# A decoder layer on one core: the attention denominators' reciprocals are spread by VectorE and DRAM transfers in place of TensorE transposes

## The chip, the cores and the metric

The kernel runs on one core of a Trainium2 chip. The metric is device time in microseconds (us) of one execution. Before the change it is 1200.84 us, the median of three runs (1200.32 to 1201.92).

## What is computed

One layer of a hybrid trunk on x of 1024 tokens by 1024 channels, float32. An RMS norm and one input projection feed two mixers: a gated DeltaNet (4 heads) and a dilated attention (8 heads of 64). Their outputs go side by side through an output projection and a residual add; then a second norm, a gated MLP with a short convolution, another residual add and the final norm.

The change is in the attention. Each of its three branches lets a query see keys at a stride; the branches are merged by their denominators, so that per head and query there is one sum of products and one sum of weights:

```python
num_tot = wts[0][..., None] * nums[0] + wts[1][..., None] * nums[1] + wts[2][..., None] * nums[2]
den_tot = wts[0] * dens[0] + wts[1] * dens[1] + wts[2] * dens[2]
out = num_tot / den_tot[..., None]
```

The kernel does all three branches as one softmax over the union of their keys (a mask holds the log of how many branches see a key), and multiplies the products by `1/den`.

## The kernel before

Activations lie with channels on the partitions and tokens along the free axis. TensorE ("PE") does the projections as dense products of split operands, three 128x512 matmuls for each 128 channels (`mm3`: `xhi,whi`, `xlo,whi`, `xhi,wlo`), and between them the pieces of whatever else is ready. A small planner (class `Weave`) runs the parts of the layer as generators: each yields an estimate of when its operands are ready, and the planner lets the one with the lowest level go on. TensorE's instructions carry a token that keeps them in the order in which they were written; the other engines' and the DMA queue's order is made by a scheduler from the order of writing, simulated times and priorities. Calls through `uv` and `ua` are VectorE ("DVE") and ScalarE ("ACT") calls with a high priority.

The attention works on two heads at a time (`pi`, 4 of them) and on half of the tokens (`hh`), which makes 8 groups, numbered 0 to 7 here. A group has four blocks of 128 queries (`u` = 0 to 3), handled in two pairs, so there are 16 pairs, numbered 0 to 15. A pair goes through three steps, and `advance` runs a step of three pairs at a time, in this order: the denominators of the older pair (`spread`), the turning of the newer one (`turn`), the values of the older one (`values`), and the scores of the next (`scores`). When the older pair is the second of its group, `merge_classes` adds the far keys, and `give` multiplies the group's products by the spread reciprocals and stores them.

- `scores` / `softmax`: products `ps<-kT,qT` in PSUM; DVE masks and takes the minimum (`sm<-ps,mk`, with `mx`), ACT takes the exponentials, which also gives the denominators `den`, two columns of the little tile `mx` (one for each head; queries are on the partitions).
- `turn`: `sm` is transposed on TensorE in 64x64 tiles (`ps<-ident,sm`, line 197; the array is used in 64 rows), and DVE and ACT copy the result to `pt` and `pb`. DVE then inverts `den` in place (`RECIPROCAL mx<-mx`), and GpSimd ("POOL") copies each of the two columns 64 times to a 128x128 tile `rd`.
- `spread`, one step later: TensorE transposes the pair's two `rd` tiles (`ps<-ident,rd`, 128x128, whole array), so that 1/den lies along the free axis on all partitions, in the PSUM bank `rb`. After the group's second pair ACT copies the bank to `rT` (`rT<-ps`).
- `give`: DVE multiplies `oT<-ps,rT`, and SyncE's queue ("SP") stores `mixer<-oT`. The last group's `oT` stays in SBUF.

Around the attention TensorE does dense columns: first `a` columns (queries and keys of later heads, stored through `apark<-aqkv`), then `z` columns, which end on DVE as `xr`, `zz` and `og`. Their weights come as `wst<-in_wi` on the SP queue, are rounded by ACT (`whi<-wst`), and the rest is made by POOL (`wlo<-wst,whi`). The SP queue also brings each pair of heads' operands (`qT`, `kT`, `vn`, `vc`). It issues in order: an issue that waits for a semaphore holds up those behind it.

Of the kernel before, what the change touches and what calls it, by code (L numbers as in the profile page):

```python
# [7 lines left out]
F32 = mybir.dt.float32  # L8
# [7 lines left out]
P = 128  # L16
# [131 lines left out]
def hybrid_layer(tc, I, out):  # L148
    nc = tc.nc
    wv = Weave()  # L150
    ve = Engine(wv, nc.vector, "vector", 0.07, 0.00105)
    ac = Engine(wv, nc.scalar, "scalar", 0.12, 0.00085)

    uv = Engine(wv, nc.vector, "vector", 0.07, 0.00105, first=tc.high_priority)
    ua = Engine(wv, nc.scalar, "scalar", 0.12, 0.00085, first=tc.high_priority)
    po_ = Engine(wv, nc.gpsimd, "gpsimd", 0.15, 0.0021)
    sy = Engine(wv, nc.sync, "sync", 0.05, 0.00142, 2.2)
# [5 lines left out]
    sp = es.enter_context(tc.tile_pool(name="sp", bufs=1))  # L163
    pp_ = es.enter_context(tc.tile_pool(name="pp", bufs=2, space=PSUM))
    dp = es.enter_context(tc.tile_pool(name="dp", bufs=1, space=DRAM))

    def tile_(pool, shape, dt, name, tag, bufs):
        return wv.slot(pool.tile(list(shape), dt, name=name, tag=tag, bufs=bufs), tag, bufs)
# [3 lines left out]
    def A(name, tag, dt=F32, shape=(P, 1024)):  # L172
        if tag in TURNS:
            i = turns[tag] = turns.get(tag, -1) + 1
            tag = TURNS[tag][i % len(TURNS[tag])]
        return tile_(lp, shape, dt, name, tag, SLOTS[tag])
# [19 lines left out]
    def tp(dst, src, idt=None, us=0.11):  # L196
        tc.stamp_issue_order_token(nc.tensor.transpose(dst, src, ident if idt is None else idt).ins, TOKEN)  # L197
        wv.product(us, dst, src)
# [60 lines left out]
    vpark = dp.tile([S, 512], F32, name="vpark")  # L259
    qpark = dp.tile([H, P, S], F32, name="qpark")  # L260
    atpark = dp.tile([H, P, S], F32, name="atpark")
    xpark = dp.tile([KT, P, S], F32, name="xpark")
    upark = dp.tile([FT, P, S], F32, name="upark")

    def bank(tag, name="ps"):
        return tile_(pp_, (P, 512), F32, name, tag, 2)
# [677 lines left out]
    HALVES = (slice(0, 64), slice(64, 128))  # L944

    def attention():
        for h in range(2):
            yield from wv.until(("c", h, NCH - 1))
        mk = A("mk", "go", shape=(P, 448))
        sy.dma_start(mk, I["mk"])  # L950
        for h in range(H):
            yield from wv.until(("o", h))
        for g in range(2):
# [43 lines left out]
        def ready_to_turn(pair):  # L997
            return max(wv.need(it["sm"], slack=t) for it, t in zip(pair, TSLACK))

        def turn(pair):  # L1000
            pts = A("pt", "dv*", shape=(P, 2, 2, 256))
            for b, (it, tag) in enumerate(zip(pair, ("asc", "atr"))):
                sm, near, far, u, den = it["sm"], it["near"], it["far"], it["u"], it["den"]
                nn, nf = near // P, -(-far // P)
                pt = it["pt"] = pts[:, b]
                pps = [bank(tag) for _ in range(2)]
                pvs = [pp.rearrange("p (e i t) -> p e i t", e=2, t=64) for pp in pps]
                for e in range(2):
                    for i in range(nn + nf):
                        o = far + i * P if i < nn else (i - nn) * P  # L1010
                        for pv, rr in zip(pvs, HALVES):
                            tp(pv[:, e, i, :], sm[rr, e, o:o + P], ident[rr, rr], 0.055)
                copies = uv.tensor_copy, lambda dst, src: ua.activation(dst, src, AF.Copy)
                for pv, rr, copy in zip(pvs, HALVES, copies):
                    copy(pt.rearrange("p e (i t) -> p e i t", t=P)[:, :, :nn, rr], pv[:, :, :nn, :])
                    for i in range(nf):
                        rows = min(it["far"] - i * P, P)
                        copy(it["pb"][i][:rows, :, u, rr], pv[:rows, :, nn + i, :])
                rd = it["rd"] = tile_(sp, [P, P], F32, "rd", ("r0", "r1", "w0", "w1")[u], 1)
                uv.reciprocal(den, den)  # L1020
                po_.tensor_copy(rd.rearrange("p (e d) -> p e d", e=2), den[:, :, None].to_broadcast([P, 2, 64]))

        def spread(pair):
            g = pair[0]["g"]
            yield wv.need(g["rb"], *[it["rd"] for it in pair])
            for it in pair:
                tp(g["rb"][:, it["u"] * P:(it["u"] + 1) * P], it["rd"])
            if pair[1]["u"] == 3:
                g["rT"] = tile_(sp, [P, 512], F32, "rT", "t2", 2)
                ac.activation(g["rT"], g["rb"], AF.Copy)  # L1030

        def values(pair):
            po = pair[0]["g"]["po"]
            yield wv.need(po, pair[0]["pt"], slack=-PSLACK)
            for it in pair:
                u = it["u"]
                for i in range(it["near"] // P):
                    for e, er in enumerate(HALVES):
                        mm(po[er, u * P:(u + 1) * P], v8(it["vn"])[:, it["k0"] // P + i, er],
                           it["pt"][:, e, i * P:(i + 1) * P], 0.11, u == 0 and i == 0, False, skip_group_check=True)  # L1040

        def merge_classes(g):
            vcv = g["vc"].rearrange("p (b c d) -> p b c d", b=2, c=4)
            po, hh = g["po"], g["hh"]
            yield wv.need(*g["pb"], slack=-PSLACK)


            parts = (((0, 128, 0), (1, 64, 2)) if hh else ((0, 64, 2),))
            for b, rows, u in parts:
                for c in range(4):  # L1050
                    for e, er in enumerate(HALVES):
                        mm(po[er].rearrange("p (u t) -> p u t", u=4)[:, u:, 32 * c:32 * c + 32],
                           vcv[:rows, b, c, er], g["pb"][b][:rows, e, u:, 32 * c:32 * c + 32], 0.11 - 0.028 * u,
                           False, c == 3 and b == hh, skip_group_check=True)

        def give(g):
            po, hh = g["po"], g["hh"]
            oT = tile_(sp, [P, 512], F32, "oT", "t2", 2)
            by = [t.rearrange("p (n c u) -> p n c u", n=4, c=4) for t in (po, g["rT"])]
            ve.tensor_tensor(oT.rearrange("p (n u c) -> p n c u", n=4, c=4), *by, op=OP.mult)  # L1060
            if g["pi"] < 3 or hh == 0:
                sy.dma_start(mixer[4 + g["pi"]][:, half(hh)], oT)
            else:
                last["oT"] = oT
            if hh == 1:
                wv.done.add(("o", 4 + g["pi"]))
# [4 lines left out]
        def advance(pair):  # L1071
            older, newer = pipe
            if newer is not None:
                yield ready_to_turn(newer)
            if older is not None:
                g = older[0]["g"]
                if older[0]["u"] == 0:
                    g.update(po=bank("ch"), rb=bank("ch"))
                yield from spread(older)
            if newer is not None:  # L1080
                turn(newer)
            if older is not None:
                yield from values(older)
                if older[1]["u"] == 3:
                    yield from merge_classes(g)
                    give(g)
            if pair is not None:
                yield from scores(pair, 0.3 if older is None else SSLACK)
            pipe[:] = newer, pair

        for pi in range(4):
            q, k, vn, vc = cur
            for hh in range(2):
                if hh == 1 and pi < 3:
                    yield from wv.until(("a", pi + 1, 1))
                    cur = att_load(pi + 1)
                pb = [A("pb", "qa", shape=(P, 2, 4, P)) for _ in range(1 + hh)]
                if pi == 3 and hh == 1:
                    wv.done.add("last group")
                for rows, b in (((slice(96, 128), 0), (slice(32, 64), 1)) if hh else ((slice(32, 64), 0),)):  # L1100
                    po_.memset(pb[b][rows, :, 0 if b < hh else 2, :], 0.0)
                g = dict(pb=pb, hh=hh, pi=pi, vc=vc)
                for u in (0, 2):
                    yield from advance([dict(n=4 * hh + i, u=i, q=q, k=k, vn=vn, pb=pb, g=g)
                                        for i in (u, u + 1)])
        for _ in range(2):
            yield from advance(None)
# [516 lines left out]
    for h in range(H):  # L1624
        wv.add(1, chain(h))
    wv.add(5, attention())
    wv.add(8, out_proj())
    wv.add(0, mixer_splits())
# [62 lines left out]
```

## Time and profile before

| | |
|---|---|
| median of the runs | 1200.84 us |
| the profiled execution's own time | 1200.36 us |
| its span, first to last instruction | 1198.6 us |
| granted TensorE clock, mean | 0.997 |
| TensorE busy | 1187.5 us, 7050 matmuls |
| VectorE / ScalarE / GpSimd busy | 915.1 / 574.8 / 89.8 us |
| attention, first turn to last merge | 322.7 to 442.8 us |

The profile is of one execution. Between its span and its time lie 1.8 us. A row of the timeline has the start and duration in us, the engine, the line, the operation, and output and inputs by the program's names; `x24` at its end means that 24 consecutive ones are merged; square brackets give the idle time of the engine before it and what ended that. PEld is TensorE's weight load, SPq the issue of a DMA on SyncE's queue. Matmuls overlap, so the distance of two starts tells what one takes, not its duration.

### The profile page before, as it was taken

How to read it: one execution, taken by the hardware profiler on the slowest of the kernel's cores; microseconds unless marked ns; L12 is line 12 of the kernel's file. 1: busy time of each engine (PE TensorE's matmuls, PEld its weight loads, DVE VectorE, ACT ScalarE, POOL GpSimd, SP SyncE). 2: the span in 40 equal slices, each digit the busy share in tenths (PEclk: the TensorE clock that was granted, in tenths of full speed). 3: DMA queues.
4: the chain of work that ended last, by engine and by line, in shares of the span. 5: the costliest groups of instructions: out<-in, count | busy, mean ns of one | idle time of the engine just before them, and what ended most of it. 6: DMA issues, size and time to landing. Idle time of an engine off the chain costs nothing.

```text
span 1198.6 us, 18324 instructions
## 1 busy us (share of the span) xinstructions
PE 1187.5 (99%) x7050; PEld 983.7 (82%) x7050; DVE 915.1 (76%) x1450; ACT 574.8 (48%) x1126; POOL 89.8 (7%) x100
## 2 busy tenths in 40 slices
PE   9999999999999999999999999999999999999997
PEld 7888888888777778888888888888888888888886
DVE  7683975665355566777989888989898889999875
ACT  7275345355454443655544544445445454434441
POOL 0212010214311120000000000000000000000000
PEclk9999999999999999999999999999999999999998
DMA  7435234436634204543213223131222398557414
GB/s 237 107 95 150 85 109 127 152 113 183 224 95 124 73 28 128 180 154 110 88 54 104 90 70 106 53 106 60 99 90 69 109 371 292 192 157 229 160 53 141
DMA packets 85798, 154.80 MB, mean 129 GB/s; under 512 B 21168, under 2 KB 36304, under 8 KB 85712
## 3 DMA queue, kind: packets, MB, share of 16 engines
q1 hardware_dynamic: 84848, 152.85, 39.1%
q8 instruction: 55, 0.90, 0.3%
q10 hardware_dynamic: 864, 0.79, 0.2%
q14 instruction: 31, 0.25, 0.1%
HBM read 117.68 MB, written 35.93 MB: 128 GB/s over the span
## 4 chain that ended last, share of the span: by engine, by line
PE 95%; DVE 2%; ACT 2%; issue 1%; DMA 0%; POOL 0%; POOLq 0%; DVEq 0%; SPq 0%; ACTq 0%
PE ps L193 45%; PE pa L193 20%; PE dw L193 17%; PE pc L193 10%; PE ps L197 3%; DVE kT L142 1%; ACT sm L144 0%; DMA xt<-in_xT 0%; DVE x1h L142 0%; ACT whi L142 0%; PE pd L193 0%; DVE zz L142 0%; ACT dec L142 0%; DVE xr L142 0%; DVE rstdB L142 0%
## 5 line engine op out<-in xcount | busy, mean ns | idle before, releaser
L193 PE MATMUL dw<-pr 128*128 128x512 f32 (+1 forms) x984 | 211.3, 376 | 0.0
L193 PEld LDWEIGHTS dw<-pr 128*128 128x128 f32 x984 | 176.7, 188 | 33.6
L193 PE MATMUL ps<-xhi,whi 128*128 128x512 f32 x384 | 157.7, 411 | 0.3 <-ACT xhi L144 0.3
L193 PE MATMUL ps<-xhi,wlo 128*128 128x512 f32 x384 | 150.3, 391 | 0.0
L193 PE MATMUL ps<-xlo,whi 128*128 128x512 f32 x384 | 148.4, 390 | 0.0
L193 PE MATMUL pa<-T,pair 128*128 128x512 f32 x528 | 127.0, 389 | 0.0
L193 PEld LDWEIGHTS pa<-T,pair 128*128 128x128 f32 x528 | 99.0, 188 | 20.6
L193 PEld LDWEIGHTS ps<-xhi,whi 128*128 128x128 f32 x384 | 72.5, 189 | 19.6 <-issue 5.6
L193 PEld LDWEIGHTS ps<-xhi,wlo 128*128 128x128 f32 x384 | 72.4, 188 | 15.7
L193 PEld LDWEIGHTS ps<-xlo,whi 128*128 128x128 f32 x384 | 72.3, 188 | 12.5
L142 ACT ACTIVATE u<-pa 128x512 f32<-128x512 f32 x44 | 26.3, 598 | 107.2 <-PE pa L193 107.2
L142 DVE SCALAR_TENSOR_TENSOR y<-xu,fcw,y 128x1023 f32<-128x1023 f32 (+1 forms) x44 | 56.4, 1281 | 22.1 <-ACT y L142 22.0
L142 ACT ACTIVATE whi<-wst 128x1024 fp32r<-128x1024 f32 x36 | 38.2, 1063 | 65.4 <-PE ps L193 54.3
L193 PE MATMUL pa<-B,A 128*128 128x512 f32 x264 | 63.4, 389 | 0.0
L193 PE MATMUL pa<-T,S 128*128 128x512 f32 x264 | 63.4, 389 | 0.0
L193 PE MATMUL pc<-B,pair 128*128 128x512 f32 x264 | 63.4, 389 | 0.0
L193 PE MATMUL pc<-T,S 128*128 128x512 f32 x264 | 63.4, 389 | 0.0
L142 DVE TENSOR_TENSOR wst<-wst 128x512 f32<-128x512 f32 x88 | 60.5, 688 | 0.9
L193 PE MATMUL ps<-B,pair 128*128 128x512 f32 x252 | 60.5, 389 | 0.0
L142 POOL TENSOR_TENSOR rs<-rs,mhalf 128x2 f32<-128x2 f32 (+2 forms) x4 | 4.7, 1187 | 738.4 <-DVE rs L144 738.4
L142 ACT ACTIVATE pr<-wd 128x1024 fp32r<-128x1024 f32 x33 | 34.9, 1058 | 49.5 <-PE dw L193 37.0
L144 ACT ACTIVATE sm<-sm,mx 128x128 f32<-128x128 f32 (+7 forms) x64 | 35.4, 556 | 48.2 <-DVE mx L144 48.2
(248 smaller groups left out, 2411.1 us busy)
## 6 DMA issues: line engine op xcount, KB each, us to landing
wst<-in_wu SPq DMA_DIRECT2D x44, 512.0 KB, 3.7
wd<-in_wd SPq DMA_DIRECT2D x44, 512.0 KB, 4.5
upark<-y SPq DMA_DIRECT2D x22, 512.0 KB, 3.6
wst<-in_wi SPq DMA_DIRECT2D x21, 512.0 KB, 3.8
r<-upark SPq DMA_DIRECT2D x11, 512.0 KB, 7.5
r<-upark SPq DMA_DIRECT2D x22, 256.0 KB, 7.5
wa<-in_wd SPq DMA_DIRECT2D x22, 256.0 KB, 3.3
wst<-in_wv SPq DMA_DIRECT2D x8, 512.0 KB, 3.7
```

The lines of the kernel that those rows point to most:

```text
L142: return getattr(eng, op)(*a, **kw)
L144: return getattr(eng, op)(*a, **kw)
L193: tc.stamp_issue_order_token(nc.tensor.matmul(dst, lhs, rhs, start=start, stop=stop, **kw).ins, TOKEN)
L197: tc.stamp_issue_order_token(nc.tensor.transpose(dst, src, ident if idt is None else idt).ins, TOKEN)
```

## The change

For groups 0 to 6 the reciprocals of both pairs go to eight columns of a 128x32 tile `dn` (two of them, in turn; the other columns hold 1.0). After the group's second pair DVE transposes `dn` to `dt` in 32x32 blocks, so that four blocks of 8 rows by 32 tokens stand on partitions 0, 32, 64 and 96. Four transfers put these side by side in DRAM as 8 rows of 128 tokens (`ddram<-dt`), and two transfers read them back, one for each head, each to 64 partitions (`rT<-ddram`). `spread` then does nothing for these groups, and `rb` is not reserved. Group 7 keeps the old way.

```diff
+    ddram = dp.tile([7, 8, P], F32, name="ddram")
...
+        dns = [tile_(sp, [P, 32], F32, "dn", f"dn{i}", 1) for i in range(2)]
+        for t in dns:
+            po_.memset(t, 1.0)
...
+                g = it["g"]
+                if g["n"] < 7:
+                    uv.reciprocal(dns[g["n"] % 2][:, 2 * u:2 * u + 2], den)
+                    continue
                 rd = it["rd"] = tile_(sp, [P, P], F32, "rd", ("r0", "r1", "w0", "w1")[u], 1)
                 uv.reciprocal(den, den)
                 po_.tensor_copy(rd.rearrange("p (e d) -> p e d", e=2), den[:, :, None].to_broadcast([P, 2, 64]))
+            g = pair[0]["g"]
+            if g["n"] < 7 and pair[1]["u"] == 3:
+                dt = tile_(sp, [P, 32], F32, "dt", "dt", 2)
+                ve.transpose(dt, dns[g["n"] % 2])
+                to = ddram[g["n"]]
+                for b in range(4):
+                    sy.dma_start(to[:, 32 * b:32 * b + 32], dt[32 * b:32 * b + 8, :])
+                rT = g["rT"] = tile_(sp, [P, 512], F32, "rT", "t2", 2)
+                for e, er in enumerate(HALVES):
+                    src = to.rearrange("(u e) t -> e u t", e=2)[e]
+                    sy.dma_start(rT[er].rearrange("p (u t) -> p u t", u=4),
+                                 bass.AP(tensor=src.tensor, offset=src.offset, ap=[[0, 64]] + list(src.ap)))
 
         def spread(pair):
             g = pair[0]["g"]
+            if g["n"] < 7:
+                return
...
-                    g.update(po=bank("ch"), rb=bank("ch"))
+                    g.update(po=bank("ch"))
+                    if g["n"] == 7:
+                        g.update(rb=bank("ch"))
...
-                g = dict(pb=pb, hh=hh, pi=pi, vc=vc)
+                g = dict(pb=pb, hh=hh, pi=pi, vc=vc, n=2 * pi + hh)
```

In the order of instructions this shows at three places. On TensorE, the turn of pair 1 (group 0), with the last dense matmuls ahead of it (`xhi`, `xlo` by `whi`, `wlo`); before:

```order
L193 MATMUL ps<-xhi,whi 128x512
L193 MATMUL ps<-xlo,whi 128x512
L193 MATMUL ps<-xhi,wlo 128x512
L197 MATMUL ps<-ident,rd 128x128 x2
L197 MATMUL ps<-ident,sm 128x64 x24
L193 MATMUL ps<-pt,vn 64x128 x6
```

and now:

```order
L193 MATMUL ps<-xhi,whi 128x512
L193 MATMUL ps<-xlo,whi 128x512
L193 MATMUL ps<-xhi,wlo 128x512
L197 MATMUL ps<-ident,sm 128x64 x24
L193 MATMUL ps<-pt,vn 64x128 x6
```

Two transposes are gone, and nothing else moved. The same holds at turns 1 to 14, so 28 transposes are gone in all; the dense matmuls ahead of each turn are as many as before.

On the SP queue, from the issue of weights ahead of group 0's transfers to group 1's; before:

```order
L142 DMA wst<-in_wi 128x1024
L142 DMA qT<-apark 128x1024
L142 DMA mixer<-oT 128x512
L142 DMA apark<-aqkv 128x1024
L142 DMA vn<-vpark 32x8x128
```

and now:

```order
L142 DMA wst<-in_wi 128x1024
L142 DMA qT<-apark 128x1024
L142 DMA ddram<-dt 8x32 x4
L142 DMA rT<-ddram 64x4x128 x2
L142 DMA mixer<-oT 128x512
L142 DMA ddram<-dt 8x32 x4
L142 DMA rT<-ddram 64x4x128 x2
L142 DMA apark<-aqkv 128x1024
L142 DMA vn<-vpark 32x8x128
```

Six transfers stand ahead of each group's store. For the later groups they also stand ahead of the next `apark<-aqkv` (groups 3 and 4) and of `wst<-in_wo` (group 6); group 2's come right behind a load of weights, `wst<-in_wi`.

On VectorE, at the last pair's turn (pair 15), where `xr`, `zz` and `og` are the end of a `z` column; before:

```order
L144 RECIPROCAL mx<-mx 128x2
L144 COPY pt<-ps 128x4x64
L144 COPY pb<-ps 128x2x64
L144 COPY pb<-ps 32x2x64
L144 COPY pt<-ps 128x4x64
L144 COPY pb<-ps 128x2x64
L144 COPY pb<-ps 64x2x64
L142 TENSOR_TENSOR oT<-ps,rT 128x4x4x32
L142 TENSOR_TENSOR xr<-ps,rstdB 128x512
L142 SCALAR_TENSOR_TENSOR zz<-zz,xr 128x1024
L142 TENSOR_TENSOR og<-og,zz 128x1024
```

and now:

```order
L144 RECIPROCAL mx<-mx 128x2
L142 TENSOR_TENSOR xr<-ps,rstdB 128x512
L142 SCALAR_TENSOR_TENSOR zz<-zz,xr 128x1024
L144 COPY pt<-ps 128x4x64
L144 COPY pb<-ps 128x2x64
L144 COPY pb<-ps 32x2x64
L142 TENSOR_TENSOR og<-og,zz 128x1024
L144 COPY pt<-ps 128x4x64
L144 COPY pb<-ps 128x2x64
L144 COPY pb<-ps 64x2x64
L142 TENSOR_TENSOR oT<-ps,rT 128x4x4x32
```

The column's end now stands ahead of the pair's copies, and `og` between those of its two blocks. TensorE shows the same: the planner put pair 15's turn, and with it the group's last products and merge, 24 dense matmuls later than before, 9 of them behind the end of that column. Elsewhere no dense matmul has changed places.

## The prediction

> **What bounds the kernel now.** I read the page first, then TensorE's timeline in the attention, then what it waits for.
>
> ```profile
> PE 1187.5 (99%) x7050; PEld 983.7 (82%) x7050; DVE 915.1 (76%) x1450; ACT 574.8 (48%) x1126; POOL 89.8 (7%) x100
> PE 95%; DVE 2%; ACT 2%; issue 1%; DMA 0%; POOL 0%; POOLq 0%; DVEq 0%; SPq 0%; ACTq 0%
> ```
>
> The first row is busy time, the second the chain of work that ended last. TensorE is busy 99% and makes up 95% of the chain. What it no longer does, it saves, unless it then waits for something else.
>
> ```profile
> L142 POOL COPY rd<-mx x32: 289/294/296, 321.6 to 436.1; 128x128 f32<-128x128 f32 x32
> L197 PE MATMUL ps<-ident,rd x32: 270/271/273, 328.3 to 440.1; 128*128 128x128 f32 x32
> L142 ACT ACTIVATE rT<-ps x8: 574/600/601, 335.3 to 440.4; 128x512 f32<-128x512 f32 x8
> ```
>
> These are the old way's instructions, by tile: 32 copies, 32 transposes, 8 copies of a bank. Seven groups of eight lose them: 28, 28 and 7.
>
> **What a pair of transposes costs TensorE.** Their 271 ns overlap, so I go by starts. Turn 0 has no `rd` ahead of it, turn 1 has:
>
> ```profile
> 322.34 0.39 PE L193 MATMUL ps<-xhi,wlo 128*128 128x512 f32 x1
> 322.66 0.59 PE L197 MATMUL ps<-ident,sm 64*128 64x64 f32 x12
> ...
> 328.10 0.40 PE L193 MATMUL ps<-xhi,wlo 128*128 128x512 f32 x1
> 328.33 0.38 PE L197 MATMUL ps<-ident,rd 128*128 128x128 f32 x2
> 328.64 0.96 PE L197 MATMUL ps<-ident,sm 64*128 64x64 f32 x24
> ```
>
> From the last dense matmul to the first `sm` transpose it is 0.54 us with the pair (328.10 to 328.64) and 0.32 without (322.34 to 322.66). So a pair saves 0.22, not the 0.31 between 328.33 and 328.64: 0.09 of that is the step from the whole array to the 64-row form (64*128 in the rows), and it then falls on the dense matmul. [...]
>
> **Where that is lost again.** The dense matmuls ahead of a turn hide the softmax of its pair, and the two `rd` transposes were part of that cover. The softmax starts at the scores, so without them a turn comes 0.22 earlier against it. Where PE already waited, nothing is gained. Turn 2 is one of the tightest of those that did not wait, turn 4 did:
>
> ```profile
> 335.11 0.17 DVE L144 RECIPROCAL mx<-mx 128x2 f32<-128x2 f32 x1
> ...
> 335.15 0.97 PE L197 MATMUL ps<-ident,sm 64*128 64x64 f32 x24
> ...
> 347.83 1.04 ACT L142 ACTIVATE whi<-wst 128x1024 fp32r<-128x1024 f32 x1
> 348.78 0.49 ACT L144 ACTIVATE sm<-sm,mx 128x256 f32<-128x256 f32 x1
> ...
> 348.87 0.88 PE L197 MATMUL ps<-ident,sm 64*128 64x64 f32 x12
> ...
> 376.94 0.89 PE L197 MATMUL ps<-ident,sm 64*128 64x64 f32 x12
> ```
>
> The reciprocal at 335.11 starts when the second block's exponentials are done. Turn 2 would now start at 334.93, and reach the second block after the first one's 12 transposes, some 0.4 later, at 335.3: still behind 335.11, no wait. Turn 4 needs 0.88 for the 12 transposes that took 0.59 at turn 0; a weight rounding on ACT (347.83) sits ahead of the last exponentials. Starting 0.22 earlier it waits 0.22 longer. Turn 8 (376.94) does the same. Turn 14 is bound by a `z` column's end:
>
> ```profile
> 420.77 1.04 ACT L142 ACTIVATE zz<-xr 128x1024 f32<-128x1024 f32 x1
> ...
> 421.84 2.56 DVE L142 SCALAR_TENSOR_TENSOR zz<-zz,xr 128x1024 f32<-128x1024 f32 x1
> 424.44 1.22 DVE L142 TENSOR_TENSOR og<-og,zz 128x1024 f32<-128x1024 f32 x1
> 425.58 0.52 DVE L144 CUSTOM_DVE_ANT_0 sm<-ps,mk 128x352 f32<-128x352 f32 x1
> ...
> 428.70 0.40 PE L197 MATMUL ps<-ident,sm 64*128 64x64 f32 x6 [0.20 <-ACT sm L144]
> ```
>
> DVE's `zz` waits for ACT's, which follows pair 13's exponentials; pair 14's softmax queues behind `zz` and `og`, and PE waits for it. From pair 13's scores to turn 14 that chain decides, so the savings at turns 13 and 14 are both lost. Four of 14 gone: 10 x 0.22 = **2.2 us**.
>
> **What the new way costs.** DVE's seven block transposes aren't in the trace; by the nearest rows they take 0.17 (a 128x2 reciprocal, 335.11) to 0.42 us (a 128x256 copy, below). They lie between the second reciprocal and the first copy, where DVE waited 0.65 for TensorE's transposes at turn 1 (below), and 0.43 with turns 0.22 earlier: hidden. The reciprocals cost what they did. POOL and ACT lose 28 x 0.29 and 7 x 0.60 that nothing waited for: 0.
>
> ```profile
> 329.26 0.42 DVE L144 COPY pt<-ps 128x256 f32<-128x256 f32 x1 [0.65 <-PE ps L197]
> ...
> 339.45 0.59 DVE L144 CUSTOM_DVE_ANT_0 sm<-ps,mk 128x416 f32<-128x416 f32 x1 [0.50 <-PE ps L193]
> ...
> 356.58 0.17 DVE L144 RECIPROCAL mx<-mx 128x2 f32<-128x2 f32 x1 [0.93 <-ACT sm L144]
> 365.93 1.09 DVE L142 TENSOR_TENSOR oT<-ps,rT 128x512 f32<-128x512 f32 x1 [0.93 <-issue]
> ...
> 384.66 0.17 DVE L144 RECIPROCAL mx<-mx 128x2 f32<-128x2 f32 x1 [0.93 <-ACT sm L144]
> ...
> 401.51 1.09 DVE L142 TENSOR_TENSOR oT<-ps,rT 128x512 f32<-128x512 f32 x1 [0.93 <-issue]
> ...
> 356.68 0.62 SPq L142 DMA_DIRECT2D wst<-in_wi  x1
> ...
> mdram<-um SPq DMA_DIRECT2D x16, 32.0 KB, 2.0
> out_xT<-x1h SPq DMA_DIRECT2D x12, 128.0 KB, 1.9
> vn<-vpark SPq DMA_DIRECT2D x16, 128.0 KB, 4.0
> dec<-gdram SPq DMA_DIRECT2D x4, 512.0 KB, 7.6
> ...
> 360.00:362.00 2.00, 2.00 (x18) 1.61 (x9) 1.90 (x8) 1.27 (x5) 0.00 (x0) 1.00 0.52 206
> 362.00:364.00 2.00, 2.00 (x31) 1.62 (x29) 1.53 (x6) 1.85 (x6) 0.59 (x2) 1.00 0.00 0
> ```
>
> The transfers must be back before `give`. Group 2's last reciprocal ends at 356.75 and its `oT` starts at 365.93: 9.2 us, 9.0 with one saving in between. A round trip on a quiet queue, as an estimate from these rows: 0.3 for transpose and semaphore, four issues of 0.32 (1.0 to the last one's start), landing like the 128-byte rows of `mdram<-um` in 2.0, the second read's issue 0.4 later, landing between 1.9 (`out_xT`) and 4.0 (`vn`, which has the same 512-byte rows, in a busy stretch). I take 2.6: **6.3 us**, bounds 5.6 and 7.7; all within 9.0. Group 2 alone meets traffic: its writes queue behind 356.68's weights, and the queue is empty from 362 (last two rows: DMA share 0.52, then 0.00). Writes landed by 362.3, reads 0.4 + 2.6 later: 365.3, with `oT` wanted at 365.7. It just fits; at 4.0 it is 1.0 late, of which DVE's idle time ahead of the next softmax takes 0.5 (339.45's row). I count 0. SP is held some 3.5 us a group; the one behind that matters, group 6's `wst<-in_wo`, is rounded no earlier than 444.94.
>
> **The last group.** Turn 15 now stands behind the end of a `z` column, with `zz` ahead of its copies on DVE:
>
> ```profile
> 436.01 0.38 PE L197 MATMUL ps<-ident,rd 128*128 128x128 f32 x2
> 440.28 1.09 PE L193 MATMUL ps<-pt,vn 128*64 128x128 f32 x16
> ...
> 444.94 1.06 ACT L142 ACTIVATE whi<-wst 128x1024 fp32r<-128x1024 f32 x1 [3.90 <-PE ps L193]
> 447.00 2.57 DVE L142 SCALAR_TENSOR_TENSOR zz<-zz,xr 128x1024 f32<-128x1024 f32 x1 [1.13 <-ACT zz L142]
> 449.60 1.23 DVE L142 TENSOR_TENSOR og<-og,zz 128x1024 f32<-128x1024 f32 x1
> ```
>
> Count from the column's end c (444.94). DVE: `zz` done at c+4.7, the first block's copies (two of 0.42) at c+5.5, `og` (1.23) at c+6.7, the second block's `pt` at c+7.1. PE: nine dense matmuls of 0.23, then 4.27 from `rd` to the last values (436.01 to 440.28): c+6.3, second block at c+6.8. It waits **0.3 us**, between 0 and 1.3 (if the first copies too come too late).
>
> **Sum:** 2.2 - 0.3 = 1.9 us off the profiled execution's 1200.36 (1.8 of it outside the span): 1198.5. The median is 0.48 above that execution, so I forecast **1198.9 us**; its own range, with two lost turns more or fewer and the 0 to 1.3, is 1198.2 to 1200.4. Under 0.2% (2.4 us) a measurement can't be told from no change, and this is 0.16%.
>
> **The rivals.** *More is saved*: the turns that wait now find ACT and DVE earlier and lose nothing, 14 x 0.22, or even the whole 0.31 a pair: 3.1 to 4.3 us, 1197.7 to 1196.5. For it, ACT's 7 x 0.60 that go; against, they stood behind the exponentials, and turn 0 shows the 0.22. Chance 0.18. *Nothing is saved*: the softmax sets the pace at most turns, not PE: 1200.8. For it, turn 2's exponentials end just 0.04 ahead of it; against, its second block comes 0.4 later. Chance 0.20. *Slower, the round trip is late*: DVE stands at `oT`, the next softmax behind it, and PE runs out of dense work. It decides from 9.0 plus DVE's 0.5 plus turn 2's 0.2: 9.7 us. The only large read in the trace that spreads DRAM rows to all partitions, `dec<-gdram`, took 7.6, for four times the bytes. With it the trip is 11.3, 1.6 late; six groups (group 4 has 16.7 us, 384.83 to 401.51) cost 9.6: 1208.5 with the other terms. Against it, the sizes: 7.6 is for 512 KB. Chance 0.12. My forecast has 0.50.
>
> The range of 1196.8 to 1201.6 leaves out the slower case and the far end of the first rival. Below 1198.4 lie the first rival and some 0.15 of the forecast's 0.50: faster 0.33; slower 0.12; same 0.55.
>
> **What would show it.** 7022 matmuls; from the last dense matmul to `sm` 0.32 at turns 1 to 14; turns 4, 8 and 14 waiting longer for ACT; `oT` starting with no wait for `rT`; a wait of 0.3 at the last values. A DVE wait for a DMA at `oT`, above all in group 2, would make it wrong, as would waits at turns 2, 6 or 10.

## The result, and the profile after

The changed kernel takes 1197.54 us (median; 1197.02 to 1199.37), the kernel before 1200.45 us beside it (1199.65 to 1201.92). The medians lie 2.9 us apart. The recorded ratio is 0.9979, with a 95% interval of 0.9969 to 0.9989: faster by 0.21%, some 2.5 us. The profiled execution took 1197.51 us, its span is 1195.7 us and its mean granted clock 0.997.

The page of the changed kernel, busy time and then the chain of work that ended last:

```profile
PE 1183.8 (99%) x7022; PEld 978.6 (82%) x7022; DVE 915.7 (77%) x1457; ACT 571.0 (48%) x1119; POOL 82.1 (7%) x74
PE 95%; DVE 2%; ACT 2%; issue 1%; DMA 0%; POOLq 0%; POOL 0%; DVEq 0%; SPq 0%; ACTq 0%
```

TensorE has 28 matmuls less and 3.7 us less busy time, and is as much the bound as it was: 99% busy, 95% of the chain. ScalarE and GpSimd lost what they were to lose.

**Where the time went.** The execution is cut at three of TensorE's matmuls that stand in every kernel here: the first transpose of `sm` (turn 0), the first product of the output projection (`ps<-ohi,whi`) and the first product of the MLP's last part (`dw<-pr`). The last mark is the first sum of squares of the final norm (`ps<-ones,sq`). First the timeline of before (its turn 0 starts at 322.66, a row shown in the prediction), then of the changed kernel:

```profile
466.74 0.39 PE L193 MATMUL ps<-ohi,whi 128*128 128x512 f32 x1
...
1189.97 0.61 PE L193 MATMUL ps<-ones,sq 128*128 128x1 f32 x4 [0.29 <-ACT sq L142]
```

```profile
321.96 0.59 PE L197 MATMUL ps<-ident,sm 64*128 64x64 f32 x12
...
463.58 0.39 PE L193 MATMUL ps<-ohi,whi 128*128 128x512 f32 x1
...
1187.19 0.61 PE L193 MATMUL ps<-ones,sq 128*128 128x1 f32 x4 [0.29 <-ACT sq L142]
```

The first `dw<-pr` starts at 976.21 before and at 973.09 after. The differences of these starts, in us, for the two kernels and for all experiments below:

| kernel | start to turn 0 | turn 0 to `ohi` | `ohi` to `dw` | `dw` to `sq` |
|---|---|---|---|---|
| before | 322.66 | 144.08 | 509.47 | 213.76 |
| after | 321.96 | **141.62** | 509.51 | 214.10 |
| after, again | 322.15 | 141.64 | 509.48 | 213.77 |
| transposes kept on TensorE | 322.12 | 143.98 | 509.47 | 213.76 |
| no transfers | 324.24 | 141.64 | 509.45 | 213.77 |
| reads twice | 322.25 | 152.49 | 509.47 | 213.98 |
| roundings behind | 322.44 | 140.86 | 509.47 | 213.76 |
| and `zz` behind | 323.13 | 140.15 | 509.48 | 213.76 |
| and `zz` behind, again | 323.47 | 140.13 | 509.48 | 213.76 |
| all eight groups | 322.03 | 140.98 | 509.46 | 214.09 |
| all three | 322.03 | 139.47 | 509.47 | 215.00 |
| all three, again | 323.08 | 139.47 | 509.45 | 214.63 |

The attention, where the change is, repeats within 0.02 us from one execution of a kernel to the next; the stretch ahead of it, in which the kernels here differ by no more than two small fills on GpSimd, scatters by 2.3 us. So the second column is what the change does: **2.46 us** saved. The profiled executions differ by 0.70 more ahead of turn 0, and the changed one lost 0.34 behind `dw`, which its repetition did not lose.

**Turn by turn.** The timeline of TensorE in the changed kernel, at turns 1, 4 and 14:

```profile
327.39 0.39 PE L193 MATMUL ps<-xhi,wlo 128*128 128x512 f32 x1
327.71 0.96 PE L197 MATMUL ps<-ident,sm 64*128 64x64 f32 x24
...
347.20 0.46 PE L197 MATMUL ps<-ident,sm 64*128 64x64 f32 x8
347.86 0.34 PE L197 MATMUL ps<-ident,sm 64*128 64x64 f32 x4 [0.20 <-ACT sm L144]
...
423.75 0.80 PE L197 MATMUL ps<-ident,sm 64*128 64x64 f32 x12
424.75 0.40 PE L197 MATMUL ps<-ident,sm 64*128 64x64 f32 x6 [0.20 <-ACT sm L144]
425.35 0.40 PE L197 MATMUL ps<-ident,sm 64*128 64x64 f32 x6 [0.20 <-ACT sm L144]
```

From the last dense matmul to `sm` it is now 0.32 (327.39 to 327.71), as at turn 0. Counted from turn 0, the start of turn 1 comes 0.23 earlier than before, turn 4 0.97, turn 8 1.77, turn 12 2.61 and turn 14 3.04. Where nothing waits, a turn gains 0.20 to 0.27, on average 0.24. Turn 4 lost 0.16 of that again, turn 8 0.13 (in the same wait), turn 14 0.38 (its first 12 transposes take 0.80, where turn 0's 12 take 0.59, and two waits of 0.20 follow), and the end of the last group 0.2. The waits view of TensorE in the attention has four waits for the exponentials, 0.8 us in all, where before had one of 0.2.

**The transfers.** In the changed kernel: VectorE's transposes by tile (least, median and largest ns); around group 2 VectorE's timeline, SP's timeline, SP's waits (total, times, longest) and the DMA issues with the median time to landing in the last column; and the waits of VectorE in the attention:

```profile
L142 DVE STREAM_TRANSPOSE dt<-dn x7: 211/211/213, 327.9 to 416.8; 128x32 f32<-128x32 f32 x7
```

```profile
355.12 0.21 DVE L142 STREAM_TRANSPOSE dt<-dn 128x32 f32<-128x32 f32 x1
...
363.88 1.09 DVE L142 TENSOR_TENSOR oT<-ps,rT 128x512 f32<-128x512 f32 x1 [0.88 <-PE ps L193]
```

```profile
354.04 1.66 SPq L142 DMA_DIRECT2D wst<-in_wi  x1
356.07 1.64 SPq L142 DMA_DIRECT2D ddram<-dt  x4
360.02 1.27 SPq L142 DMA_DIRECT2D rT<-ddram  x2
```

```profile
SPq L142 <- DMA ddram<-dt: 2.2, 1, 2.2
```

```profile
rT<-ddram SPq DMA_DIRECT2D x2, 128.0 KB, 2.9
```

```profile
DVE oT L142 <- PE ps L193: 9.8, 7, 2.1
```

In this execution every one of the seven `oT` that use transferred reciprocals waits for TensorE's products, none for `rT`. Group 2 is the tight one: 0.95 from the transpose to the first write's issue behind the weights, SP then waits 2.2 for the writes to land, and the second read, issued near 360.7, lands 2.9 later, about 8.5 us after the transpose began. `oT` starts 8.76 after it. There were some 0.3 us to spare.

That was luck. In the eight other profiles that have these transfers and each read once, the repetition of this kernel among them, group 2's `oT` waits for `rT`: 1.00 to 1.75 us, where the products end a wait of 0.88, and it starts 8.90 to 9.65 after the transpose. VectorE's timeline in the repetition, and then the next softmax in the execution above:

```profile
364.73 1.10 DVE L142 TENSOR_TENSOR oT<-ps,rT 128x512 f32<-128x512 f32 x1 [1.53 <-DMA rT<-ddram]
365.68 0.57 DVE L144 CUSTOM_DVE_ANT_0 sm<-ps,mk 128x416 f32<-128x416 f32 x1
```

```profile
365.42 0.59 DVE L144 CUSTOM_DVE_ANT_0 sm<-ps,mk 128x416 f32<-128x416 f32 x1 [0.45 <-PE ps L193]
```

In the repetition `rT` is 0.65 late. VectorE's idle time of 0.45 ahead of the next softmax is gone, and turn 7 still starts 47.23 after turn 0, against 47.22: so small a delay cost TensorE nothing.

### The profile page after: what moved, and what is told of

It reads as the page before. It is cut to its first block, busy times and chain, and to the rows that moved or that the text cites. A ratio compares the mean times of both kernels' runs of the same rounds, so it can differ in the third digit from the quotient of the medians.

```text
span 1195.7 us, 18255 instructions
## 1 busy us (share of the span) xinstructions
PE 1183.8 (99%) x7022; PEld 978.6 (82%) x7022; DVE 915.7 (77%) x1457; ACT 571.0 (48%) x1119; POOL 82.1 (7%) x74
## 4 chain that ended last, share of the span: by engine, by line
PE 95%; DVE 2%; ACT 2%; issue 1%; DMA 0%; POOLq 0%; POOL 0%; DVEq 0%; SPq 0%; ACTq 0%
PE ps L193 45%; PE pa L193 20%; PE dw L193 17%; PE pc L193 10%; PE ps L197 2%; DVE kT L142 1%; ACT sm L144 1%; ACT whi L142 0%; DMA xt<-in_xT 0%; DVE x1h L142 0%; PE pd L193 0%; DVE zz L142 0%; ACT dec L142 0%; DVE xr L142 0%; DVE sm L144 0%
## 5 line engine op out<-in xcount | busy, mean ns | idle before, releaser
L142 ACT ACTIVATE pr<-r 128x1024 fp32r<-128x1024 f32 (+1 forms) x44 | 36.2, 838 | 45.7 <-PE dw L193 31.3
L193 PEld LDWEIGHTS pa<-T,S 128*128 128x128 f32 x264 | 49.5, 188 | 10.3
L193 PEld LDWEIGHTS pc<-B,pair 128*128 128x128 f32 x264 | 49.5, 188 | 10.3
```

The lines of the kernel that those rows point to most:

```text
L142: return getattr(eng, op)(*a, **kw)
L193: tc.stamp_issue_order_token(nc.tensor.matmul(dst, lhs, rhs, start=start, stop=stop, **kw).ins, TOKEN)
```

## Experiments

**Is the start the change's?** The changed kernel once more.

> The changed kernel once more, for a second profile. In the first profiles its turn 0 came 0.70 us earlier than that of the kernel before, though nothing ahead of it was changed but two small fills on GpSimd. Theory (the first matmuls run at a varying rate from execution to execution): turn 0 falls anywhere between 321.9 and 322.7 us, and from turn 0 to the first dense matmul behind turn 14 the difference to before stays 2.6 to 2.7 us. Rival (the change itself makes the start faster): turn 0 again at 321.9 to 322.0.

Measured: 1197.53 us, ratio 0.9977 (0.9967 to 0.9988). Turn 0 starts at 322.15, between the two earlier profiles, so this run by itself decides nothing on the start. The table does, with the others: the changed kernel and the kernels made from it have turn 0 anywhere between 321.96 and 324.24, and before's 322.66 lies between them. The 0.70 can't be told from the scatter of the start, and isn't counted as a gain. From turn 0 to `ohi` it is the same again, 141.64.

**Is the gain TensorE's time, or the relief of ACT and POOL?** All is as in the changed kernel, but at each place where a pair of `rd` was transposed, TensorE transposes a constant identity into a bank that nobody reads. POOL's and ACT's copies stay away.

```diff
             if g["n"] < 7:
+                for it in pair:
+                    dst = g["rx"][:, it["u"] * P:(it["u"] + 1) * P]
+                    tc.stamp_issue_order_token(nc.tensor.transpose(dst, ident, ident).ins, TOKEN)
                 return
...
+                    else:
+                        g.update(rx=pp_.tile([P, 512], F32, name="rx", tag="ch", bufs=2))
```

> The changed kernel with two transposes of the constant identity put back on TensorE at each of turns 1 to 14, to a bank that nobody reads; VectorE, ScalarE, GpSimd and the transfers stay as changed. Theory (what is gained is TensorE's time for the 28 transposes): 2.5 to 3.1 us slower than the changed kernel, 1200.0 to 1200.6, ratio to before 0.9995 to 1.0000. Rival (what is gained is ScalarE's and GpSimd's relief): as fast as the changed kernel, 1197.5, ratio 0.998.

Measured: 1200.10 us, ratio 0.9999 (0.9990 to 1.0008). TensorE's timeline of this kernel at turn 1:

```profile
327.55 0.40 PE L193 MATMUL ps<-xhi,wlo 128*128 128x512 f32 x1
327.79 0.38 PE L1048 MATMUL rx<-ident 128*128 128x128 f32 x2
328.10 0.96 PE L197 MATMUL ps<-ident,sm 64*128 64x64 f32 x24
```

0.55 from the dense matmul to `sm`, as before the change. The attention takes 143.98: of the 2.46 us 2.36 are gone, and the time is that of before. The gain is TensorE's time. All else that the change does, the end of POOL's and ACT's copies included, comes to the remaining 0.10.

**Do the transfers cost anything?** The writes and reads are left out, and the seven products are multiplied by another tile instead: attention's division by the denominators is missing for groups 0 to 6.

```diff
-                    sy.dma_start(to[:, 32 * b:32 * b + 32], dt[32 * b:32 * b + 8, :])
...
-            by = [t.rearrange("p (n c u) -> p n c u", n=4, c=4) for t in (po, g["rT"])]
+            by = [t.rearrange("p (n c u) -> p n c u", n=4, c=4) for t in (po, g["rT"] if "rT" in g else rstdB[:, :512])]
```

> The changed kernel without the six transfers of groups 0 to 6; their give multiplies by another tile that lies ready (so the attention's division is left out). Reciprocals and block transposes stay. Theory (the transfers are hidden): 1197.5, within 0.3 us of the changed kernel, and the same spacing of the turns. Rival (42 transfers on the in-order SP queue and the wait for their return cost something): faster than the changed kernel by 1 us or more, ratio to before 0.997 or less.

Measured: 1198.85 us (1197.03 to 1200.43), ratio 0.9984 (0.9974 to 0.9994). That is no faster than the changed kernel, and the attention takes 141.64, 0.02 from the changed kernel's. The 42 transfers cost nothing, and that holds where group 2's are late, too: the repetition of the changed kernel takes 141.64 as well. That the median is 1.3 higher isn't explained by anything behind turn 0: in the profile it all lies ahead of it (324.24, the latest start of the table). Why the timed runs of this kernel lie so high was not settled.

**How much room is there?** The two reads are issued twice, with the same content.

```diff
+                for e, er in enumerate(HALVES):
+                    src = to.rearrange("(u e) t -> e u t", e=2)[e]
+                    nc.sync.dma_start(rT[er].rearrange("p (u t) -> p u t", u=4),
+                                      bass.AP(tensor=src.tensor, offset=src.offset, ap=[[0, 64]] + list(src.ap)))
```

> The changed kernel with the two reads of each group done twice, one after the other, which makes each round trip some 3.7 us longer. Theory (there is little to spare, and a late round trip costs TensorE time through VectorE standing at give): the spare time of groups 0, 1, 2, 3, 5 and 6 was 1.2, 3.0, 0.3, 2.9, 1.2 and 4.5 us, so groups 0, 2 and 5 come 2.5, 3.4 and 2.5 us late, 1 and 3 0.7; less some 0.7 us that VectorE and TensorE have to spare each, 6 to 7 us slower than the changed kernel: 1204, ratio 1.003. Rival (VectorE's stand is absorbed by the dense matmuls): 1197.5 to 1198.5, ratio 0.998 to 0.999.

Measured: 1208.05 us, ratio 1.0065 (1.005 to 1.008): 10.5 us slower than the changed kernel beside it, more than expected. The attention takes 152.49, 10.87 more. In this kernel: the waits of VectorE in the attention, TensorE's timeline in group 2, and the stretches around it (busy time of PE, PEld, DVE, ACT and POOL, granted clock, DMA share, GB/s):

```profile
DVE oT L142 <- DMA rT<-ddram: 22.6, 5, 7.7
```

```profile
371.48 0.39 PE L193 MATMUL ps<-xhi,wlo 128*128 128x512 f32 x1
375.70 0.58 PE L197 MATMUL ps<-ident,sm 64*128 64x64 f32 x6 [3.83 <-ACT sm L144]
```

```profile
371.00:373.00 2.00, 0.87 (x4) 0.38 (x2) 0.00 (x0) 0.00 (x0) 0.00 (x0) 1.00 0.22 67
373.00:375.00 2.00, 0.00 (x0) 0.00 (x0) 1.67 (x4) 0.09 (x1) 0.00 (x0) 0.79 0.00 0
375.00:377.00 2.00, 1.30 (x18) 1.04 (x18) 1.49 (x7) 2.00 (x7) 0.00 (x0) 0.50 0.35 131
...
379.00:381.00 2.00, 2.00 (x18) 1.67 (x16) 0.46 (x4) 0.09 (x1) 0.00 (x0) 0.51 0.01 2
381.00:383.00 2.00, 2.00 (x11) 1.41 (x10) 1.98 (x10) 1.62 (x7) 0.00 (x0) 1.00 0.36 107
```

The trips grew by more than the 3.7 us expected: group 2's `oT` starts 15.0 after its transpose (358.32 to 373.33), 6.3 later than in the changed kernel. This is the prediction's slower rival at work: VectorE stands at `oT` for `rT` in five of seven groups, the next softmax queues behind it, and TensorE runs out. Group 2 (turn 5 to turn 8) costs 7.6 of the 10.87 us: a stall of 3.8, and then a granted clock of 0.50 to 0.51 until 381. TensorE's work from 375.70 to 381.0, 5.3 us, went at that clock: 16 products `ps<-pt,vn` took 1.97 us (at 378.25), where 16 of the same size take 1.09 in the changed kernel (at 425.67). By the clock that is another 2.6 of the 5.3, an estimate. That second part is in no expectation. The 0.79 of 373 to 375 gives an estimate of when the clock fell: with 1.00 up to that point and 0.50 from there, as in the stretches on either side, it is at about 374.2, some 2.3 us after TensorE's last work (375.70 less 3.83 is 371.87).

**Can the turns that lost be mended?** At turns 4 and 8 a weight rounding on ACT stands ahead of the pair's last exponentials. Here it goes behind the exponentials that have been written last.

```diff
-            ac.activation(hi, st, AF.Copy)
+            inst = ac.activation(hi, st, AF.Copy)
+            if "exp" in last:
+                after(inst, last["exp"], "the softmax goes first")
```

> The changed kernel with the weight roundings on ScalarE (whi<-wst) kept behind the last exponentials written before them. This moves two of them, at turns 4 and 8, where one stood ahead of the last exponential; nothing else moves but one pair of neighbouring transfers. Theory (that rounding is what TensorE waits for there, 0.4 us each): turns 4 and 8 take 0.55 instead of 0.95 us from their first transpose to the first of the values, 0.8 us less in all, 1196.7, ratio to before 0.997. Rival (the weights then come late for the next column, or the exponentials wait for VectorE anyway): no gain, 1197.5.

Measured: 1196.67 us, ratio 0.9972 (0.9961 to 0.9983). Turn 4 on TensorE, and ACT ahead of it, in this kernel:

```profile
347.68 0.59 PE L197 MATMUL ps<-ident,sm 64*128 64x64 f32 x12
```

```profile
346.76 0.49 ACT L144 ACTIVATE sm<-sm,mx 128x256 f32<-128x256 f32 x1
...
347.25 1.04 ACT L142 ACTIVATE whi<-wst 128x1024 fp32r<-128x1024 f32 x1
```

The rounding (347.25) follows the exponentials, and the 12 transposes take 0.59 again, without a wait. The attention takes 140.86, 0.76 less, 0.4 at each of the two turns. That is more than the 0.16 and 0.13 that the change lost there, since the turns had waited before it, too.

**Turn 14.** In addition, the end of the `z` column (`zz`, `og`) waits for the masks of pair 14's softmax.

```diff
+                def end(h=h, og=og, zz=zz, xr=xr):
+                    if h == 0:
+                        yield from wv.until("scored")
+                    ac.activation(zz, xr, AF.Tanh, scale=0.5)
+                    inst = ve.scalar_tensor_tensor(zz, zz, 1.0, xr, op0=OP.add, op1=OP.mult)
+                    if h == 0:
+                        after(inst, last["mask"], "the softmax goes first")
+                    ve.tensor_tensor(og, og, zz, op=OP.mult)
```

> The kernel of the run before, with zz of the first z column kept behind the masks of pair 14's softmax on VectorE, so that the softmax does not queue behind zz and og; three dense matmuls change places with pair 14's scores on TensorE. Theory (turn 14's 1.8 us of transposes, where 0.9 would do, come from that queue): 0.9 us less from turn 13 to the dense matmuls behind turn 14, 1195.8. Rival (the chain over ScalarE's rounding, tanh and copies holds pair 14's scores as well, which now come earlier): at most 0.3 us less.

Measured: 1195.61 us, ratio 0.9966 (0.9953 to 0.9978). VectorE's timeline of this kernel, and TensorE's at turn 14:

```profile
422.15 0.55 DVE L144 CUSTOM_DVE_ANT_0 sm<-ps,mk 128x384 f32<-128x384 f32 x1
...
422.63 1.22 DVE L142 SCALAR_TENSOR_TENSOR zz<-zz,xr 128x1024 f32<-128x1024 f32 x1
```

```profile
423.78 0.96 PE L197 MATMUL ps<-ident,sm 64*128 64x64 f32 x24
```

`zz` follows the last mask, the 24 transposes take 0.96 with no wait, and the attention gets another 0.71 shorter (0.9 were expected).

**The last group.** All eight groups go through DRAM (without the two edits above): `ddram` gets an eighth entry, and the bounds of 7 become 8.

```diff
-                if g["n"] < 7:
+                if g["n"] < 8:
                     uv.reciprocal(dns[g["n"] % 2][:, 2 * u:2 * u + 2], den)
...
-                    if g["n"] == 7:
-                        g.update(rb=bank("ch"))
```

> The changed kernel with group 7 on the new way too, so that no transposes of reciprocals are left and the bank rb is never needed; the planner then puts turn 15 where it stood in the kernel before. Theory (two more pairs of transposes at 0.22 to 0.31 us, and no wait at the last values): 0.5 to 0.7 us less than the changed kernel, 1196.9, ratio to before 0.9972. VectorE waits at group 7's give for the transfers, some 3 us, but the end of the z column behind it comes later than that. Rival (that wait holds VectorE and with it the z column's end): not faster, or slower by up to 2 us.

Measured: 1196.88 us, ratio 0.9973 (0.9963 to 0.9983). The attention takes 140.98, 0.64 less than in the changed kernel, though VectorE now waits for a transfer:

```profile
439.10 1.07 DVE L142 TENSOR_TENSOR oT<-ps,rT 128x512 f32<-128x512 f32 x1 [3.97 <-DMA rT<-ddram]
...
441.45 0.69 DVE L142 TENSOR_TENSOR xr<-ps,rstdB 128x512 f32<-128x512 f32 x1 [1.28 <-PE ps L193]
```

This wait of 3.97 costs nothing: no softmax is left behind it, and the next work, `xr`, waits for TensorE all the same. Here, too, a late transfer cost only what stood behind it.

**All three edits.**

> The three edits of the runs before together. Theory: they lie at different turns and add up, 0.8 + 0.9 + 0.6 = 2.3 us less than the changed kernel, 1195.2, ratio to before 0.9958. Rival: if the second gains nothing, 1196.1.

Measured: 1196.16 us (1194.92 to 1198.24), ratio 0.9968 (0.9959 to 0.9978), and not the 1195.2 expected. The attention did what the sum said: 139.47, that is 2.15 less than the changed kernel, where the three make 0.76 + 0.71 + 0.64 = 2.11. But 1.24 were lost behind `dw`. So this kernel and the one without the third edit were run again beside each other.

> The same kernel as the one with the zeroing of `zz` behind the masks and the weight roundings behind the exponentials, run again beside the next one. In the profiles so far, counted from turn 0, it ends 1.6 us ahead of the changed kernel, and the kernel with all three edits was 2.6 us ahead at the end of attention but gave 0.9 us back at 972 us, where TensorE waited 0.92 us for `xu` behind a late read of `upark`. Theory A (the late read belongs to that one execution): this kernel's median lies 0.5 to 1.1 us above that of the kernel with all three. Theory B (the read is a floor in every execution, so that what is gained ahead of it is lost there): the two medians lie within 0.3 us. Time expected here: 1195.8.

> The kernel with all three edits again. Theory A: 1194.9, no wait over 0.3 us at 972 in its profile, `pr<-r` starts near 970.3. Theory B: 1195.7, the wait of 0.9 us for `xu` is there again and `pr<-r` starts near 971.1 again.

Measured: 1196.17 us (1195.69 to 1197.16; ratio 0.9967, 0.9955 to 0.998) and 1195.64 us (1195.28 to 1197.04; 0.9962, 0.9948 to 0.9975). The attentions repeat, 140.13 and 139.47, and the loss behind `dw` is there again, 0.87. In the kernel with all three, ScalarE's timeline and TensorE's:

```profile
971.80 1.06 ACT L142 ACTIVATE pr<-r 128x1024 fp32r<-128x1024 f32 x1 [4.32 <-DMA r<-upark]
972.76 0.58 ACT L142 ACTIVATE xu<-pa 128x512 f32<-128x512 f32 x1
```

```profile
972.00 0.84 PE L193 MATMUL dw<-pr 128*128 128x512 f32 x3
973.39 2.80 PE L193 MATMUL dw<-pr 128*128 128x512 f32 x11 [0.55 <-ACT xu L142]
```

`xu` stands on ACT behind `pr<-r`, which waits for a read of DRAM, and TensorE needs `xu`. In the first profile of this kernel TensorE waits 0.92 for `xu` in the same place, but there the profile puts the wait of `pr<-r` (971.13) down to TensorE's `pc`, so the read is shown as the cause in the repetition only. ACT in the kernel without the third edit, and then in the changed kernel:

```profile
971.71 1.06 ACT L142 ACTIVATE pr<-r 128x1024 fp32r<-128x1024 f32 x1 [3.15 <-DMA r<-upark]
```

```profile
972.37 1.06 ACT L142 ACTIVATE pr<-r 128x1024 fp32r<-128x1024 f32 x1 [3.81 <-DMA r<-upark]
```

Without the third edit the read is in at 971.71, while the first `dw` is at 973.08, 1.1 later than with it: the read was not earlier when TensorE was. In the changed kernel's first profile `pr<-r` came 0.72 ahead of `dw` and 0.34 was lost; 1.76 ahead in its repetition, and nothing was. So what seems to count is how late `pr<-r` is against TensorE. Theory A does not stand as put, since the wait was there both times; theory B's floor fits both traces, but the medians differ by 0.53, more than it allows, and their intervals cover each other. What sets the start of `pr<-r`, and how often a kernel that is 2 us earlier loses 1 us there, stays open, as does the 0.33 that the kernel with all eight groups lost behind `dw`.

Of the versions run, the one with roundings and `zz` behind and the one with all three are the fastest, 1195.6 to 1196.2 us; neither is shown to be ahead of the other.

## Why the prediction was right, and where it was not

**TensorE's time is the gain**: right. Putting the 28 transposes back took 2.36 of 2.46 us away.

**0.22 us a pair**: it is 0.24 on average, 3.3 in place of 3.1. The step of 0.09 us into the 64-row form did stay and now lies on the dense matmul: 0.32 from 327.39 to 327.71, where the dense matmuls ahead start 0.23 apart (327.16 to 327.39). A saving of the whole 0.31 falls.

**Four turns lose it, 0.88 in all**: mis-sized, 0.67. At turns 4 and 8 the cause was right, the rounding, as the edit that takes it away showed, but 0.16 and 0.13 were lost, not 0.22. The step that failed is that "the savings at turns 13 and 14 are both lost": turn 14 starts a full 0.23 earlier against turn 13, with no wait ahead of its first transpose, and then loses 0.38 among its transposes, which wait for exponentials. The chain named, `zz` ahead of the softmax on VectorE, was the right one, as the edit that turns the two round showed.

**The transfers are free**: right, by the run without them, to 0.02 us, but not because all were back in time. The quiet trip was sized well: group 1's took 6.1 us (transposed at 341.74, the reads issued from 344.26, the second landed near 347.8), where 6.3 were taken. Group 2's was put at 8.5 us (356.75 to 365.3), with 0.4 to spare. It took 8.5 in the first profile, with 0.3 to spare, and more in each of the eight others, where `rT` came 0.1 to 0.9 late. What kept it free there is the other half of the prediction's argument, that VectorE's idle time ahead of the next softmax and TensorE's cover take up a delay until 9.7 us: the latest `oT` with each read done once starts 9.65 after its transpose, and the kernel with roundings and `zz` behind has the same attention with 9.15 in one execution and 9.54 in the other (140.15 and 140.13). The part that was too small is the landing of the writes, taken as 2.0: SP waited for it 2.2 us after the last issue in the first profile and 3.0 in the repetition. The margin is thin: with the reads doubled, the slower rival came about.

**The last group's 0.3**: 0.2 were lost between turn 14 and the output projection.

Together the attention saved 2.46 where 1.9 was forecast. Of the 1.36 us between the forecast's 1198.9 and the measured 1197.54, that is 0.56; another 0.39 is the base, since the three runs that it was laid on had a median of 1200.84, and the kernel before has 1200.45 beside the change. The rest is within the scatter of the runs. The stated range, 1196.8 to 1201.6, holds the time before as well as the time after, so it shows little that the time lies in it; what the traces bear out is the account by turns. A change under 0.2% was held the likeliest, at 0.55; it is 0.21%, and the interval of the ratio, 0.9969 to 0.9989, doesn't reach 1.

**The rivals.** The time lies in the stretch that "more is saved" was given (1196.5 to 1197.7), but its reason is not what happened: turns 4, 8 and 14 wait more than before, not less, a pair doesn't save the whole 0.31, and not every pair's saving is kept. "Nothing is saved" fell at turn 1. "Slower" had the mechanism right and the trip too long: with each read done once it stayed under the 9.7 us from which a delay was to cost something.

**What would show it**: 7022 matmuls, 0.32 at the turns and the longer waits at turns 4, 8 and 14 came, and 0.2 of the 0.3 at the last values. `oT` without a wait for `rT` came in the first profile only. The wait for a DMA at group 2's `oT`, which was to make the prediction wrong, came in the eight others and cost nothing, so that sign was set too strictly: it should have named a delay past 9.7 us.

## What to carry to other kernels

Where one engine was busy 99%, moving its small work to transfers paid what the distances of its starts showed. The transfers were free as long as their round trip, issue waits and landing of the small writes included, ended before the first use, or so little behind it that idle time took up the delay: it took 6.1 us in a quiet group, 8.5 and more in the one that met traffic, and with the reads doubled it was no longer free. One profile doesn't show that a transfer is in time: the first was the only one of nine without a wait for `rT`. Look in the same profile for what shares a queue with the work that will now come earlier, since the roundings and `zz` that stood ahead of a softmax cost 1.5 us, more than half of what the change gained. And measure a small gain between two instructions of the trace around the change: that repeated within 0.02 us, where whole executions differ by 2.

## What was not expected of the hardware

**The start.** First the timeline of before, then of the changed kernel, then of the kernel without transfers, where line numbers are 6 higher:

```profile
6.67 0.63 PE L193 MATMUL ps<-xhi,whi 128*128 128x512 f32 x1
7.10 0.46 PE L193 MATMUL ps<-xhi,wlo 128*128 128x512 f32 x1
7.40 0.39 PE L193 MATMUL ps<-xhi,whi 128*128 128x512 f32 x1
7.63 0.40 PE L193 MATMUL ps<-xhi,wlo 128*128 128x512 f32 x1
```

```profile
5.97 0.39 PE L193 MATMUL ps<-xhi,wlo 128*128 128x512 f32 x1
6.20 0.40 PE L193 MATMUL ps<-xhi,whi 128*128 128x512 f32 x1
```

```profile
10.25 0.60 PE L199 MATMUL ps<-xhi,wlo 128*128 128x512 f32 x1
10.68 0.41 PE L199 MATMUL ps<-xhi,whi 128*128 128x512 f32 x1
10.92 0.40 PE L199 MATMUL ps<-xhi,wlo 128*128 128x512 f32 x1
```

A dense matmul takes 0.43 us at first (6.67 to 7.10) and 0.23 later (7.40 to 7.63). The step comes at about 7 us in the first, ahead of 6 us in the second, and not before 10.5 us in the third, though the same work stands there. So the step is shown, and a scatter of over 4 us; what makes it isn't, since the profiles have a granted clock of 1.00 from 0 to 12 us. Waits for the first inputs add to it (1.58 us for `xhi` in one execution, 0.34 in another). The two executions of the kernel with roundings and `zz` behind waited 1.0 and 1.1 us for `sq` ahead of turn 0 and have it at 323.13 and 323.47; before waited 0.2 and has it at 322.66. In all, turn 0 scatters over 2.3 us.

**The clock after a stall.** In the kernel with doubled reads the granted clock fell to 0.50 within a gap of 3.8 us of TensorE, some 2.3 us into it, and the 5.3 us of work at 0.50 to 0.51 behind it cost a further 2.6; both are the estimates above. The changed kernel has such a fall at its end, 0.76 from 1188 to 1189 and 0.50 from there, where TensorE's gap is 1.10. What sets the fall was not shown.
